# First two chunks of the two 4096-wide feed-forward nets: weights stationary and one tile's 128 tokens moving

## The chip, the cores and the metric

The kernel is one program on one core of a Trainium2 chip. The metric is the device time of one execution in microseconds (us): the median of 3 runs before is 1135.75 us (1135.49 to 1136.52).

The core has a matrix engine (PE in the profile; its weight loads are shown apart, as PEld), a vector engine (DVE), a scalar engine (ACT), GpSimd (POOL) and an engine that issues DMAs (SP). Each takes its own instructions in the order in which the program put them, and waits on semaphores for the others. A matmul multiplies a stationary operand, 128x128, which a weight load brings into the array, by a moving operand of up to 512 columns, and adds the result into a PSUM bank of 128x512 floats.

## The reference, cut to what matters

Three blocks run one after the other on 256 tokens of width 1024, all in float32: a mixer block with a gated net of width 2816, a retention layer, and an attention layer. Retention and attention are each followed by a net of width 4096 with a squared ReLU; these two nets are what the change touches:

```
D_FF_2 = 4 * D_MODEL
def sq_relu_mlp(x, w_up, w_down):
    h = jax.nn.relu(x @ w_up)
    return (h * h) @ w_down
h = h + rms_norm(sq_relu_mlp(rms_norm(h, mpre), w_up, w_down), mpost)
```

## The kernel before

**Split numbers.** Every float32 operand of a large product is split into two rounded parts (type float32r), a high part and the rest. ACT writes the high part, DVE the rest (`split`, L683). A product is then three matmuls, high by high, high by rest and rest by high (`mm3`, L540). The weights come by DMA into `raw` tiles in units of two k-tiles by 512 columns or one k-tile by 1024, 512 KB each; the split puts them into `whi` and `wlo`, of which there are eight buffers each. The activations lie split and transposed (features on the partitions, 256 tokens along the row) in `y8` tiles, named y in the profile. `Parts` (L351) keeps them so that the high and the low part of one k-tile lie side by side.

**Two ways to multiply.** `rows_proj` (L546) has 128 tokens stationary and 512 weight columns moving: 8 k-tiles by three matmuls of 512 columns. Its result has tokens on the partitions, so `rows_T` (L698) transposes it in four 128x128 matmuls against an identity (`const`) and splits it. `cols_proj` (L555) has 128 weight columns stationary; a first matmul moves the high and low parts of all 256 tokens (512 columns) past the high weights, a second moves the high part alone (256 columns) past the rest. Its result is already transposed. `two_blocks` (L564) does two such blocks and adds the two halves.

**The nets.** `run_mlp` (L1223) cuts the 4096 hidden columns into eight chunks of 512. The first two (`ROWS_FIRST`) go through `up` with `token_rows`: for each of the two token tiles (t), for each chunk, a projection by rows, the squared ReLU and the transposes. The reason for the row form there is in the loop: work on tile 0 begins while the input of tile 1 (normalised, transposed and split by `next_T`, L1134) is still being made; `flush()` (L1374) records that before tile 1's work. Chunks 2 to 7 use `two_blocks`. The transposes of the input of tile 1 are matmuls too: 8 of 128x128, in two groups of four.

**What sets the order.** The kernel is recorded twice. In the first pass `Plan` (L69) schedules all operations by its own costs and due times; in the second they are issued in that order, so each engine's queue is fixed. Its cost for a float32r matmul (L197) prices a moving operand of under 256 columns at four times the rate of a wider one:

```
if ins[0].dtype == F32R:
    return n * 0.4167e-3 * (1 if n >= 256 else 4) + 0.0027
```

The kernel before has no float32r matmul of under 256 columns. The four PSUM banks named `mx` are handed out in the order of first use, so the transposes of tile 1's input wait for the first bank that the chunk results leave.

Of the kernel before, what the change touches and what calls it, by code (L numbers as in the profile page):

```python
# [27 lines left out]
AF = mybir.ActivationFunctionType  # L28
OP = mybir.AluOpType
# [4 lines left out]
KT = D // 128  # L34
# [302 lines left out]
class Part:  # L337
# [5 lines left out]
    def __getitem__(self, at):  # L343
        p, k, c = at if len(at) == 3 else (*at, slice(None))
        if isinstance(k, int):
            return self.tiles[k // 4][p, k % 4, self.s, c]
        n = (k.start or 0) // 4
        return self.tiles[n][p, (k.start or 0) - 4 * n:k.stop - 4 * n, self.s, c]


class Parts:  # L351
# [5 lines left out]
    def __getitem__(self, s):  # L357
        if s > 1:
            raise IndexError
        return Part(self.tiles, s)  # L360

    def both(self, k):
        return self.tiles[k // 4][:, k % 4].rearrange("p s n -> p (s n)")
# [3 lines left out]
def network(ctx, tc, I, consts, c_at, out, after=None):  # L367
    nc = tc.nc
    plan = Plan(after)
    V, S, T, G, Q = [Engine(plan, n, e) for n, e in (("DVE", nc.vector), ("ACT", nc.scalar), ("PE", nc.tensor),  # L370
                                                     ("POOL", nc.gpsimd), ("SP", nc.sync))]
# [5 lines left out]
    def sbt(shape, tag, bufs, dt=F32):  # L377
        return plan.tile(sb, shape, dt, tag, bufs)

    def pj():  # L380
        return plan.tile(ps, [128, 512], F32, "pj", 4)

    def mx():
        return plan.tile(ps, [128, 512], F32, "mx", 4)
# [7 lines left out]
    def t2():  # L392
        return sbt([128, 512], "t2", 6)
# [4 lines left out]
    def f32(ap):  # L398
        return ap.bitcast(F32)
# [6 lines left out]
    def cols(a, n):  # L406
        return a.rearrange("p (a b) -> p a b", b=n)
# [93 lines left out]
    def pump(upto):  # L501
        while state["split"] <= min(upto, len(units) - 1) and state["split"] < state["done"] + NSPL:
            i = state["split"]
            load_to(i + NRAW - 1)
            src, kt, n, deint, gain = units[i]
            raw = raws.pop(i)
            hi = sbt([128, UNIT], "whi", NSPL, F32R)[:, :kt * n]
            lo = sbt([128, UNIT], "wlo", NSPL, F32R)[:, :kt * n]
            if deint:
                src4 = raw.rearrange("p (k m c) -> p k c m", k=kt, c=2)  # L510
                hi4, lo4 = [a.rearrange("p (k c m) -> p k c m", k=kt, c=2) for a in (hi, lo)]
                for k in range(kt):
                    S.activation(hi4[:, k], src4[:, k], AF.Copy)
                    V.tensor_tensor(lo4[:, k], src4[:, k], f32(hi4[:, k]), op=OP.subtract)
            elif gain is not None:
                for k in range(kt):
                    split(hi[:, k * n:(k + 1) * n], lo[:, k * n:(k + 1) * n], raw[:, k * n:(k + 1) * n],
                          g_col[:, gain + k:gain + k + 1])
            else:
                split(hi, lo, raw)  # L520
            spl[i] = (cols(hi, n), cols(lo, n))
            state["split"] += 1
        load_to(state["split"] + NRAW - 1)

    def weight(key):
        i = index[key]
        pump(i + AHEAD)
        return spl[i]
# [7 lines left out]
    def release_chunk(key, n):  # L536
        for j in range(n):
            release((key, j))

    def mm3(acc, x, w, first, last):  # L540
        T.matmul(acc, x[0], w[0], start=first, stop=False)
        T.matmul(acc, x[0], w[1], start=False, stop=False)
        T.matmul(acc, x[1], w[0], start=False, stop=last)


    def rows_proj(key, hT, t, acc, c0, n, per=2, nk=KT):  # L546
        for j in range(nk // per):
            w = weight((key, j))
            for k in range(per):
                kk = j * per + k  # L550
                x_ = [a[:, kk, t * 128:(t + 1) * 128] for a in hT]
                mm3(acc, x_, [a[:, k, c0:c0 + n] for a in w], kk == 0, kk == nk - 1)
# [11 lines left out]
    def two_blocks(key, hT, pool, c0, per=2, nk=KT):  # L564
        ps_ = pool(), pool()
        for b, p in enumerate(ps_):
            cols_proj(key, hT, p, c0 + b * 128, per, nk)
        s = cols(t2(), 256)
        for b, p in enumerate(ps_):
            S.activation(s[:, b], p[:, 256:], AF.Copy)  # L570
            V.tensor_tensor(s[:, b], p[:, :256], s[:, b], op=OP.add)
        return s
# [47 lines left out]
    col, n = {}, 0  # L620
# [62 lines left out]
    def split(hi, lo, src, scale=None):  # L683
        if scale is None:
            S.activation(hi, src, AF.Copy)
            V.tensor_tensor(lo, src, f32(hi), op=OP.subtract)
        else:
            S.activation(hi, src, AF.Copy, scale=scale)
            V.scalar_tensor_tensor(lo, src, scale, f32(hi), op0=OP.mult, op1=OP.subtract)

    def new_hT():
        return Parts([y8(), y8()])

    def new_y():
        return Parts([y8()])


    def rows_T(src, dst, k0, t, nb=4, scale=None):  # L698
        p = cols(mx(), 128)[:, :nb]
        for j in range(nb):  # L700
            T.transpose(p[:, j], src[:, j * 128:(j + 1) * 128], ident)
        hi, lo = [a[:, k0:k0 + nb, t * 128:(t + 1) * 128] for a in dst]
        split(hi, lo, p, scale)
# [153 lines left out]
    hT = new_hT()  # L857
# [10 lines left out]
    for key in ("fq", "fk"):  # L868
        heads[key] = cols(p4(), 256)
        acc = pj(), pj()  # L870
        for j in range(4):
            w = weight((key, j))
            for t in range(2):
                for k in range(2):
                    kk = 2 * j + k
# [72 lines left out]
    for t in range(2):  # L948
        p = pj()
# [56 lines left out]
    for t in range(2):  # L1006
        p = pj()
# [12 lines left out]
        for c in range(2 - t):  # L1020
            r = slice(c * 64, (c + 1) * 64)
# [4 lines left out]
        for i in range(2):  # L1026
            r = slice(i * 64, i * 64 + 64)
            V.tensor_copy(qm[r, i::2, t, 0::3], tp[r, :2].rearrange("p a (c n) -> p a c n", c=2))
        tk = slice(t * 128, (t + 1) * 128)
# [15 lines left out]
    for c in range(3):  # L1045
        cs = cols(mx(), 256)
        for pr in range(2):
            T.matmul(cs[:, pr], koz[:, c, pr * 128:(pr + 1) * 128], gv[:, c // 2, pr * 256:(pr + 1) * 256],
                     start=True, stop=True)
        for i in range(2):  # L1050
            r = slice(i * 64, i * 64 + 64)
            if c == 0:
                V.tensor_copy(stt[r, 0], cs[r, :, i * 128:(i + 1) * 128])
            else:
                for pr in range(2):
                    cc = cs[r, pr, i * 128:(i + 1) * 128]
                    V.scalar_tensor_tensor(stt[r, c, pr], stt[r, c - 1, pr], decay[r, 4 * pr + c:4 * pr + c + 1], cc,
                                           op0=OP.mult, op1=OP.add)
    y_gla = new_y()
    for t in range(2):  # L1060
        tk = slice(t * 128, (t + 1) * 128)
        op = mx()
# [15 lines left out]
        for j in range(4):  # L1078
            V.scalar_tensor_tensor(y_gla[1][:, j, tk], tp[:, j], ggla[:, j:j + 1], f32(y_gla[0][:, j, tk]),
                                   op0=OP.mult, op1=OP.subtract)  # L1080
# [5 lines left out]
    for n, i in enumerate(BR):  # L1086
        for c in range(2):
            gt = cols(p4(), 256)
            for b2 in range(2):
                p = two_blocks(("gate", i, c), hT, pj, 256 * b2)  # L1090
# [8 lines left out]
            for b2 in range(2):  # L1099
                p = two_blocks(("br", i, c), ys[i], pj, 256 * b2, nk=4)  # L1100
                g2 = gt[:, 2 * b2:2 * b2 + 2]
                m = mg[c][:, 2 * b2:2 * b2 + 2]
# [5 lines left out]
                if n == 2:  # L1108
                    k = slice(4 * c + 2 * b2, 4 * c + 2 * b2 + 2)
# [62 lines left out]
    def flush():  # L1172
        while later:
            later.pop(0)()

    g_ffn = halves(gain_rows("g_ffn"))
    hT = new_hT()
# [88 lines left out]
    hT = hT_n  # L1266
# [89 lines left out]
    hT = hT_n  # L1356

    def sq_relu(p):  # L1360
        r = t2()
        S.activation(r, p, AF.Relu)
        V.scalar_tensor_tensor(r, p, 0.0, r, op0=OP.max, op1=OP.mult)
        return r

    def sq_up(l):
        key = f"up{l}"

        def up(cs, token_rows):
            aT = {c: new_y() for c in cs}  # L1370
            if token_rows:
                for t in range(2):
                    if t:
                        flush()  # L1374
                    for c in cs:
                        p = mx()
                        rows_proj((key, c), hT, t, p, 0, 512)
                        rows_T(sq_relu(p), aT[c], 0, t)
            else:
                for c in cs:  # L1380
                    for b2 in range(2):
                        p = two_blocks((key, c), hT, mx, 256 * b2)
                        V.scalar_tensor_tensor(p, p, 0.0, p, op0=OP.max, op1=OP.mult)
                        m = slice(2 * b2, 2 * b2 + 2)
                        split(aT[c][0][:, m], aT[c][1][:, m], p)
            for c in cs:
                release_chunk((key, c), 4)
            return aT
        return up
# [16 lines left out]
    hT = hT_n  # L1406
# [62 lines left out]
    hT = hT_n  # L1469
# [56 lines left out]
```

## Time and profile before

| | |
|---|---|
| median of 3 runs | 1135.75 us (1135.49 to 1136.52) |
| the profiled execution, its time | 1135.74 us |
| the profiled execution, first to last instruction (span) | 1134.0 us |
| PE busy | 1124.5 us, 99% |
| DVE busy | 822.3 us, 73% |
| ACT busy | 649.8 us, 57% |
| granted TensorE clock, mean | 0.999 |

The span is what the rows are measured in; 1.7 us of the execution lie outside it. A row of the timeline merges neighbours of one form: start, length from the first start to the last end, form, count. Matmuls are pipelined and each is shown with its latency, so the pace of a series is read from starts, or from a merged row as its length less one matmul's mean duration, divided by the count less one.

### The profile page before, as it was taken

Reading aid. Unit: us, or ns where it says so; the run is one execution under the profiler, and the core shown is the slowest. Engines: PE = TensorE matmul, PEld = TensorE weight load, DVE = VectorE, ACT = ScalarE, POOL = GpSimd, SP = SyncE. Lnnn points to the kernel's source line nnn. Section 1 sums busy time; section 2 is a strip of 40 time slices with the busy share of each in tenths; the row PEclk is TensorE's granted clock in tenths of the full one; section 3 lists DMA queues with packets and bytes.
Section 4 is the critical chain, followed back from the end, with each engine's and each line's share of the span. In section 5 each row is a group of like instructions: output and inputs, shape, how many; then the busy total and the mean of one; then the engine's idle time right before and its main releaser. Section 6 shows DMA issues by size and latency. Waiting matters only on the chain.

```text
span 1134.0 us, 15708 instructions
## 1 busy us (share of the span) xinstructions
PE 1124.5 (99%) x5756; PEld 948.0 (84%) x5756; DVE 822.3 (73%) x1487; ACT 649.8 (57%) x1068; POOL 6.0 (1%) x18
## 2 busy tenths in 40 slices
PE   9999999999999999999999999999999999999997
PEld 7989888888888888888888888888888888888885
DVE  7998797897656566787858497656588889755564
ACT  6867657675645554646556474545466667645451
POOL 1000000000000000000000000000000000000000
PEclk9999999999999999999999999999999999999999
DMA  8654545675666664665464458564637354655631
GB/s 296 222 163 125 165 134 182 220 223 176 205 187 197 186 190 129 201 205 189 150 204 163 130 170 279 167 206 154 217 115 255 117 173 141 225 197 181 215 112 38
DMA packets 100883, 204.22 MB, mean 180 GB/s; under 512 B 6661, under 2 KB 30278, under 8 KB 100806
## 3 DMA queue, kind: packets, MB, share of 16 engines
q1 hardware_dynamic: 99942, 202.17, 55.1%
q10 hardware_dynamic: 864, 1.05, 0.3%
q8 instruction: 45, 0.74, 0.3%
q14 instruction: 32, 0.26, 0.1%
HBM read 202.14 MB, written 1.05 MB: 179 GB/s over the span
## 4 chain that ended last, share of the span: by engine, by line
PE 98%; DVE 1%; DMA 0%; ACT 0%; SPq 0%; issue 0%; DVEq 0%; ACTq 0%
PE pj L213 64%; PE mx L213 34%; DMA raw<-in_w_in_dram 0%; DVE p L213 0%; DVE sm L213 0%; DVE wlo L213 0%; SPq L213 0%; ACT t L213 0%; ACT whi L213 0%; DVE y L213 0%; DVEq L1515 0%; ACTq L213 0%
## 5 line engine op out<-in xcount | busy, mean ns | idle before, releaser
L213 PE MATMUL pj<-whi,y 128*128 128x512 f32 (+2 forms) x1744 | 543.7, 388 | 0.0
L213 DVE TENSOR_TENSOR wlo<-raw,whi 128x1024 fp32r<-128x1024 f32 (+1 forms) x326 | 377.7, 1169 | 125.9 <-ACT whi L213 121.5
L213 ACT ACTIVATE whi<-raw 128x1024 fp32r<-128x1024 f32 (+1 forms) x326 | 326.9, 1018 | 123.2 <-PE pj L213 92.1
L213 PEld LDWEIGHTS pj<-whi,y 128*128 128x128 f32 x1744 | 321.7, 188 | 66.1 <-issue 0.3
L213 PE MATMUL pj<-wlo,y 128*128 128x512 f32 (+2 forms) x872 | 337.4, 387 | 0.7 <-DVE wlo L213 0.6
L213 PE MATMUL mx<-y,whi 128*128 128x512 f32 x672 | 236.8, 396 | 0.0
L213 PEld LDWEIGHTS pj<-wlo,y 128*128 128x128 f32 x872 | 164.0, 188 | 33.5 <-DVE wlo L213 1.8
L213 PE MATMUL mx<-y,wlo 128*128 128x256 f32 x672 | 188.5, 281 | 0.0
L213 PEld LDWEIGHTS mx<-y,whi 128*128 128x128 f32 x672 | 126.1, 188 | 30.0
L213 PE MATMUL pj<-y,whi 128*128 128x512 f32 x416 | 146.4, 396 | 0.0
L213 PEld LDWEIGHTS mx<-y,wlo 128*128 128x128 f32 x672 | 126.5, 188 | 0.9
L213 PE MATMUL pj<-y,wlo 128*128 128x256 f32 x416 | 116.5, 280 | 0.0
L213 PEld LDWEIGHTS pj<-y,whi 128*128 128x128 f32 x416 | 78.1, 188 | 18.2
L213 ACT ACTIVATE t<-mx 128x256 f32<-128x256 f32 (+1 forms) x106 | 41.5, 396 | 83.0 <-PE mx L213 80.4
L213 DVE SCALAR_TENSOR_TENSOR wlo<-raw,gcol,whi 128x512 fp32r<-128x512 f32 (+2 forms) x120 | 85.0, 746 | 5.4 <-ACT whi L213 3.7
L213 ACT ACTIVATE whi<-raw,gcol 128x512 fp32r<-128x512 f32 (+2 forms) x120 | 79.8, 716 | 14.7 <-PE pj L213 10.8
L213 PEld LDWEIGHTS pj<-y,wlo 128*128 128x128 f32 x416 | 78.3, 188 | 0.1
L213 DVE TENSOR_TENSOR t<-mx,t 128x256 f32<-128x256 f32 x88 | 37.0, 421 | 52.3 <-ACT t L213 52.3
L213 PE MATMUL mx<-whi,y 128*128 128x512 f32 x192 | 61.5, 396 | 0.0
L213 ACT ACTIVATE t<-pj 128x256 f32<-128x256 f32 (+1 forms) x74 | 29.7, 402 | 55.5 <-PE pj L213 42.2
L213 ACT ACTIVATE y<-t 128x512 fp32r<-128x512 f32 x33 | 20.9, 632 | 45.0 <-DVE t L213 45.0
L213 PE MATMUL mx<-const,t 128*128 128x128 f32 (+1 forms) x295 | 45.0, 272 | 0.0
(143 smaller groups left out, 839.5 us busy)
## 6 DMA issues: line engine op xcount, KB each, us to landing
raw<-in_w_in_dram SPq DMA_DIRECT2D x115, 512.0 KB, 4.5
raw<-in_w_up_dram SPq DMA_DIRECT2D x64, 512.0 KB, 4.6
raw<-in_w_down_dram SPq DMA_DIRECT2D x64, 512.0 KB, 4.9
raw<-in_w_out_dram SPq DMA_DIRECT2D x32, 512.0 KB, 4.2
raw<-in_w_ffn_down_dram SPq DMA_DIRECT2D x22, 512.0 KB, 3.6
raw<-in_w_ffn_gate_dram SPq DMA_DIRECT2D x18, 512.0 KB, 3.8
raw<-in_w_ffn_up_dram SPq DMA_DIRECT2D x18, 512.0 KB, 5.1
raw<-in_w_branch_dram SPq DMA_DIRECT2D x12, 512.0 KB, 4.7
```

The source lines that it names most:

```text
L213: self.ops[i]()
```

## The change

In the two 4096-wide nets the first two chunks no longer go through `rows_proj` and `rows_T`. A new helper `tile_blocks` takes one token tile and 256 hidden columns: for each of two blocks of 128 weight columns and each of 8 k-tiles, one matmul moves the tile's 128 tokens, high and low part (256 columns), past the high weights, and one moves the high part alone (128 columns) past the rest. Both blocks share one PSUM bank. ACT then copies one half out, DVE adds the other, squares with the ReLU, and the result is split; there are no transposes. The helper is called twice for each chunk and tile. The gated net is not touched, nor are chunks 2 to 7.

```diff
+    def parts(self, k):
+        return self.tiles[k // 4][:, k % 4]
...
-    def sq_relu(p):
-        r = t2()
-        S.activation(r, p, AF.Relu)
-        V.scalar_tensor_tensor(r, p, 0.0, r, op0=OP.max, op1=OP.mult)
-        return r
+    def tile_blocks(key, c, b2, t, y):
+        tk = slice(t * 128, (t + 1) * 128)
+        p = mx().rearrange("p (b s n) -> p b s n", b=2, s=2)
+        for b in range(2):
+            c0 = 256 * b2 + 128 * b
+            for kk in range(KT):
+                wb = [a[:, kk % 2, c0:c0 + 128] for a in weight(((key, c), kk // 2))]
+                T.matmul(p[:, b], wb[0], hT.parts(kk)[:, :, tk], start=kk == 0, stop=False)
+                T.matmul(p[:, b, 0], wb[1], hT[0][:, kk, tk], start=False, stop=kk == KT - 1)
+        u = cols(t2()[:, :256], 128)
+        S.activation(u, p[:, :, 1], AF.Copy)
+        V.tensor_tensor(u, p[:, :, 0], u, op=OP.add)
+        V.scalar_tensor_tensor(u, u, 0.0, u, op0=OP.max, op1=OP.mult)
+        m = slice(2 * b2, 2 * b2 + 2)
+        split(y[0][:, m, tk], y[1][:, m, tk], u)
...
                     for c in cs:
-                        p = mx()
-                        rows_proj((key, c), hT, t, p, 0, 512)
-                        rows_T(sq_relu(p), aT[c], 0, t)
+                        for b2 in range(2):
+                            tile_blocks(key, c, b2, t, aT[c])
```

The planned order of the queues changes with it. On PE, at the first of the two nets, the transposes of tile 1's input (here from t2_1173 and t2_1174) stood after 34 matmuls of 512 columns, eight together with the first four of the chunk result (t2_1168). Before:

```order
L213 MATMUL mx_86<-whi_1162,y8_1110 128x512 [waits Activation_49]
L213 MATMUL mx_86<-wlo_1163,y8_1110 128x512 [waits DVE_49]
L213 MATMUL mx_86<-whi_1162,y8_1110 128x512 x2
L213 MATMUL mx_83<-const_64,t2_1173 128x128 [waits DVE_49]
L213 MATMUL mx_83<-const_64,t2_1173 128x128 x3
L213 MATMUL mx_90<-const_64,t2_1168 128x128 x4
L213 MATMUL mx_86<-wlo_1163,y8_1110 128x512
```

After, at the same place (the same transposes now read t2_1175 and t2_1176):

```order
L213 MATMUL mx_90<-y8_1111,whi_1153 128x256
L213 MATMUL mx_90<-y8_1111,wlo_1154 128x128
L213 MATMUL mx_83<-const_64,t2_1175 128x128 [waits DVE_49]
L213 MATMUL mx_83<-const_64,t2_1175 128x128 x3
L213 MATMUL mx_90<-y8_1111,whi_1153 128x256
L213 MATMUL mx_90<-y8_1111,wlo_1154 128x128
```

The first group now stands after 42 matmuls (16 pairs into bank mx_83 and 5 pairs into mx_90), and the second group follows 10 matmuls, or 5 pairs, later; both go into mx_83. In the second net the counts are the same, 42 and 10.

On DVE, the same place in the first net: the queue that ends the making of tile 1's input and then takes the first chunk result out of bank mx_83. Before:

```order
L213 SCALAR_TENSOR_TENSOR t2_1173<-t2_1173,sm_1180,p4_1094 128x512 [waits DVE_49]
L213 SCALAR_TENSOR_TENSOR t2_1174<-pj_97,sm_1180,p4_1092 128x512
L213 TENSOR_TENSOR t2_1174<-t2_1174,p4_1094 128x512 [waits DVE_49]
L213 SCALAR_TENSOR_TENSOR t2_1168<-mx_83,t2_1168 128x512 [waits Activation_49]
L213 TENSOR_TENSOR wlo_1170<-raw_1152,whi_1169 128x1024 [waits DMAHW1_49,PE_49]
L213 TENSOR_TENSOR p4_1144<-p4_1144,p4_1090 128x1024
```

After:

```order
L213 SCALAR_TENSOR_TENSOR t2_1175<-t2_1175,sm_1182,p4_1094 128x512 [waits DVE_49]
L213 SCALAR_TENSOR_TENSOR t2_1176<-pj_97,sm_1182,p4_1092 128x512
L213 TENSOR_TENSOR t2_1176<-t2_1176,p4_1094 128x512 [waits DVE_49]
L213 TENSOR_TENSOR t2_1168<-mx_83,t2_1168 128x256 [waits Activation_49]
L213 TENSOR_TENSOR wlo_1171<-raw_1152,whi_1170 128x1024 [waits DMAHW1_49]
L213 SCALAR_TENSOR_TENSOR t2_1168<-t2_1168 128x256 [waits DVE_49]
L213 TENSOR_TENSOR y8_1110<-mx_83,y8_1110 128x4x128 [waits Activation_49]
```

The operation that empties mx_83 (t2_1168<-mx_83) still stands behind the same three operations on tile 1's input; it is half as wide, and one weight split and the square stand between it and the operation that empties mx_83 a second time (y8_1110<-mx_83).

## Rows read from the trace of the kernel before

**Rows 1.** The page: span, PE's busy time, and the chain's shares by engine.

```profile
span 1134.0 us, 15708 instructions
PE 1124.5 (99%) x5756; PEld 948.0 (84%) x5756; DVE 822.3 (73%) x1487; ACT 649.8 (57%) x1068; POOL 6.0 (1%) x18
...
PE 98%; DVE 1%; DMA 0%; ACT 0%; SPq 0%; issue 0%; DVEq 0%; ACTq 0%
```

**Rows 2.** The chain in order of time, first net: start us, us, what.

```profile
655.32 36.10 PE mx L213 x184
691.41 22.12 PE pj L213 x96
```

**Rows 3.** Timeline of PE, the first net's row stage: start us, us, form, count.

```profile
655.15 0.39 PE L213 MATMUL mx<-whi,y 128*128 128x512 f32 x1
...
663.01 1.04 PE L213 MATMUL mx<-const,t 128*128 128x128 f32 x8
...
665.98 0.60 PE L213 MATMUL mx<-const,t 128*128 128x128 f32 x4
...
666.65 0.62 PE L213 MATMUL mx<-whi,y 128*128 128x512 f32 x2
...
679.60 0.39 PE L213 MATMUL mx<-y,whi 128*128 128x512 f32 x1
```

**Rows 4.** Busy us (x instructions) in both nets' row stages; the second's first matmul.

```profile
655.16:679.60 24.44, 24.44 (x118) 19.95 (x117) 23.28 (x42) 18.20 (x31) 0.00 (x0) 1.00 0.43 141
945.51:969.90 24.39, 24.39 (x118) 20.02 (x116) 23.49 (x40) 17.31 (x31) 0.00 (x0) 1.00 0.47 150
...
945.51 0.40 PE L213 MATMUL mx<-whi,y 128*128 128x512 f32 x1
```

**Rows 5.** Timeline of PE: float32r matmuls of 256 columns back to back.

```profile
92.52 0.27 PE L213 MATMUL pj<-wlo,y 128*128 128x256 f32 x1
...
93.34 0.28 PE L213 MATMUL pj<-whi,y 128*128 128x256 f32 x1
```

**Rows 6.** PE, 128 moving columns (plain float32): a timeline row, then all by form.

```profile
123.50 1.05 PE L213 MATMUL mx<-y,p 128*128 128x128 f32 x8
...
L213 PE MATMUL mx<-y,p 128*128 128x128 f32 x16 | 2.1, 275 | 0.0
```

**Rows 7.** Weight loads by form (busy us, mean ns), then two neighbours in the timeline.

```profile
L213 PEld LDWEIGHTS pj<-whi,y 128*128 128x128 f32 x1744 | 321.7, 188 | 66.1 <-issue 0.3 <-ACT whi L213 0.3
L213 PEld LDWEIGHTS mx<-const,t 128*128 128x128 f32 x294 | 36.0, 140 | 8.3 <-DVE t L213 1.0
...
649.74 0.19 PEld L213 LDWEIGHTS pj<-whi,y 128*128 128x128 f32 x1
649.85 0.19 PEld L213 LDWEIGHTS pj<-wlo,y 128*128 128x128 f32 x1
```

**Rows 8.** Timeline of DVE, first net, while tile 1's input is made.

```profile
661.61 0.69 DVE L213 TENSOR_TENSOR t<-t,p 128x512 f32<-128x512 f32 x1
662.22 0.68 DVE L213 SCALAR_TENSOR_TENSOR t<-mx,t 128x512 f32<-128x512 f32 x1
662.82 1.21 DVE L213 TENSOR_TENSOR wlo<-raw,whi 128x1024 fp32r<-128x1024 f32 x1
663.95 1.22 DVE L213 TENSOR_TENSOR p<-p,p 128x1024 f32<-128x1024 f32 x1
```

**Rows 9.** Timeline of DVE, the same place of the second net.

```profile
945.90 0.68 DVE L213 TENSOR_TENSOR y<-mx,y 128x512 fp32r<-128x512 f32 x1
...
952.15 0.69 DVE L213 SCALAR_TENSOR_TENSOR t<-mx,t 128x512 f32<-128x512 f32 x1
```

**Rows 10.** DVE and ACT by form: busy us, mean ns, idle before.

```profile
L213 DVE TENSOR_TENSOR t<-mx,t 128x256 f32<-128x256 f32 x88 | 37.0, 421 | 52.3 <-ACT t L213 52.3
...
L213 DVE TENSOR_TENSOR y<-mx,y 128x512 fp32r<-128x512 f32 x44 | 29.7, 684 | 4.1 <-ACT y L213 4.0
...
L213 ACT ACTIVATE t<-mx 128x256 f32<-128x256 f32 x96 | 35.6, 375 | 75.3 <-PE mx L213 75.3
```

## The prediction

> **What bounds the kernel now.** I read the page first. PE is busy for 99% of the span, and the chain that ends last runs on PE for 98% [rows 1]: whatever PE has to do more or less of goes straight into the time, and work of the other engines counts only where PE waits for it. So the case is one of PE's pace in two short stretches, and of the waits that a new order brings there.
>
> The stretches are the row stages of the two wide nets, 24.44 and 24.39 us, both with PE filled to the end at the full granted clock (1.00, the 2.4 GHz level) [rows 4]. What fills them can be counted. 96 matmuls of 512 columns take 22.12 us, or 0.2304 each [rows 2]. Four transposes with one such matmul behind them take 666.65 - 665.98 = 0.67 us, so the four alone 0.44 [rows 3]. In the first stage stand 96 matmuls and 20 transposes: 22.12 + 5 x 0.44 = 24.32 of 24.44 us. There is next to no wait to win. DVE is busy for 23.28 of these 24.44 us [rows 4], close behind, but PE does not wait for it.
>
> **What it removes.** For each net 96 matmuls of 512 columns, 22.12 us, and 16 transposes (four of them after the stage), 4 x 0.44 = 1.76. Together 23.88 us on the path.
>
> **What it adds on PE.** For each net 2 chunks x 2 tiles x 4 blocks x 8 k-tiles = 128 pairs: a matmul of 256 columns and one of 128, each with a weight load of its own.
>
> The 256: seven back to back take 93.34 - 92.52 = 0.82 us, 0.117 each [rows 5].
>
> The 128 is what decides, and the trace has none in this type. Bounds from the nearest rows: at the low end half of the 256, 0.058 (columns alone count); at the high end the 0.2304 of a 512 [rows 2], which is the planner's assumption of a quarter of the rate. Between them stands the nearest real row, the plain float32 matmuls of 128 columns with a load each: eight in 1.05 us, one lasting 275 ns, so (1.05 - 0.275) / 7 = 0.111 each [rows 6]. I take this value, for the load speaks for it whatever the moving side can do: two loads of this type, neither held up by a long matmul, start 649.74 and 649.85, that is 0.11 apart [rows 7], and I take it that a load hides behind one matmul, the one before its own. Behind a 256 (0.117) it just fits; behind a 128 it does not. So the change moves as many columns as before (128 x 384 = 96 x 512) in 256 loads instead of 96, and half of these loads set the pace.
>
> A pair is then 0.117 + 0.111 = 0.228 us, 128 pairs 29.18, and each net's stage grows by 29.18 - 23.88 = 5.3 us. Both: **+10.6 us**.
>
> The Trainium skill speaks against this change in the same sense: "TensorE: Matmul & The Clock Gate", section "LDWEIGHTS (loading the stationary operand)", has a load take as long as its columns at 1.2 GHz, 107 ns for 128 by its formula, whatever moves. The trace agrees with its 0.11 [rows 7]; by the page's figure in place of 0.111 the growth would be an estimated 4.8 us a net instead of 5.3.
>
> **The new order's waits.** The queues are fixed by a plan that prices the 128 at four times its width, so the plan reaches each point later than PE will. The first transposes of tile 1's input now stand after 42 matmuls, 21 pairs: at my pace 4.79 us into the stage, at 655.15 + 4.79 = 659.94 [rows 3]. They need bank mx_83, which DVE empties only behind the three operations on tile 1's input; these do not get shorter, since they start from the previous layer's last product. In the trace DVE gets past them at 662.22, empties the bank in 0.68 us to 662.90, and the transposes begin at 663.01 [rows 3, 8], with no gap on PE, because 34 matmuls of 0.23 had brought it there at the same moment. Now the emptying takes 0.42 [rows 10]: 662.22 + 0.42 + 0.11 = 662.75. PE waits **2.8 us**, and all that is queued behind the transposes on PE waits with it.
>
> The second group goes into the same bank, 5 pairs later: PE is there at 662.75 + 0.44 + 1.14 = 664.33. Before it DVE has a weight split, the square (256 wide) and the split of the first group: with neighbours overlapping by some 0.07 [rows 8], 662.22 + 0.35 + 1.13 + 0.35 + 0.68 = 664.73, and 664.84 with the hand-over. **0.5 us**.
>
> Second net: the upper half of tile 0's input is needed after 4 pairs (945.51 + 0.91 = 946.42 [rows 4]) where 12 long matmuls stood before; DVE ends it at 946.58 [rows 9], so 0.3 us with the hand-over. Then 945.51 + 0.3 + 4.79 = 950.6 against 952.15 + 0.42 + 0.11 = 952.68 [rows 9, 10]: 2.1. The second group as above: 0.5. In all 3.3 us in the first net and 2.9 in the second, **+6.2 us**. This is an estimate from rows of an order that is no longer there; if DVE frees the bank earlier the waits go to 0, and at worst I give them half as much again.
>
> **What costs nothing.** Emptying and splitting a chunk result costs DVE more: three operations of 0.42 for half a chunk (2.5 for a whole one) instead of 0.68 + 0.68 [rows 10], about 1.2 x 4 = 4.6 us a net, and ACT some 1.4. DVE then has 23.3 + 4.6 = 27.9 us of work in a stage of 29.2 + 3.3 = 32.5; without that slack (a pair under 0.19) PE would begin to wait for it. The weight buffers come free later, since every unit is read four times and not once for each tile; between the last read of chunk 0 and the start of chunk 2 lie some 9 us, in which ACT and DVE have four splits of 1.1 to do. The DMAs of the weights have the same bytes to bring in more time.
>
> **Sum.** The profiled execution took 1135.74 us, at the median (1135.75). 1135.74 + 10.6 + 6.2 = **1152.5 us**. With no waits it is 1146.3; with waits of 9 and a pair dearer by 0.01 (256 x 0.01 = 2.6), 1158.
>
> **The rivals.**
>
> *A quarter of the rate.* The 128 streams no faster than a 512. For it: no row has this type at this width, so nothing excludes it, and the planner's cost assumes it. The 0.111 is also for one of the two instructions into which a plain float32 product falls (16 rows for the kernel's 8 such products [rows 6]). Against it: the assumption has no row behind it either. Priced as both of those instructions, 2 x 0.111 = 0.222: 128 x 0.339 = 43.4, less 23.88, is 19.5 a net, 39.0 in both. PE then reaches the transposes at 655.15 + 7.12 = 662.27, so the waits shrink to some 0.5 in all: 1175.2. At 0.2304 it is 1176.9.
>
> *The load hides further.* The loads of transposes are shorter (140 ns against 188) [rows 7]; were this type's so too, a pair would near 0.117 + 0.058 = 0.175, 22.4 us a net, 3.0 less in both. But PE would be at the first transposes at 658.8 and wait 3.9 us, then 0.9; second net 4.4: -3.0 + 9.2, and DVE becomes the bound for another 1 or 2 us: 1143. So even the low end of the matmul's cost is slower than before. Against it: the two loads 0.11 apart. The skill's page has a rule to this side (section "Back-to-back issue gap"): 81 ns for a matmul of 128 in a stream with loads. By it I estimate 1147.
>
> *Not slower.* The low end, 0.175 a pair, and bank mx_83 free when PE asks, because the emptying is reached earlier than at 662.22. That gives 1135.74 - 3.0 = 1132.7. It decides from a pair of 0.187 with no wait at all (23.88 / 128), and needs both that DVE skips a chain which the order keeps and that a load takes under 0.07. Very little speaks for it.
>
> **How the numbers follow.** Load-bound pairs with waits: 0.61, 1152.5, itself 1146 to 1158. A quarter of the rate: 0.30, 1175 to 1177. The load hides: 0.06, 1143. Not slower: 0.03, 1132.7. The likeliest gives the time. The first two hold 0.91; to hold 8 in 10 the range has to reach the second, so it runs from 1145 to 1177. About 0.2% (2.3 us) is what a measurement can tell from no change. All cases but the last are slower by more; of its 0.03, two thirds faster and one third same, and a little more for same from waits and pairs both at their low ends: faster 0.02, same 0.02, slower 0.96.
>
> **What would show it.** Right: 128 matmuls of each width in each of the two stages, starts 0.11 to 0.12 apart throughout, weight loads at the same pace, stages of about 32.5 and 32.1 us, and one gap on PE of 2 to 3 us before the first transposes, put down to DVE. Wrong in the size of the 128: starts 0.22 or more behind each of them, a stage of some 44 us and no gap (A quarter), or 0.06 to 0.08 (the load hides). Wrong in the waits: no gap, with the bank emptied before 660. Everything outside the stages should keep its length, 22.12 us for the 96 matmuls behind among it.

## The result

The changed kernel took 1155.67 us at the median of 4 runs (1153.81 to 1156.45), the kernel before beside it 1136.13 (1135.49 to 1137.36): 1.0168 times as long, interval 1.0156 to 1.018, or 19.5 us. A second set of runs gave 1155.33 against 1135.97. The forecast was 1152.5, range 1145 to 1177, slower with a chance of 0.96. The sign and the mechanism of the pairs held. The median lies 3.2 us above the forecast, and most of these 3.2 us have a cause that the prediction did not name at all, a fall of PE's clock; the experiments isolate it.

The profiled execution of after is the quickest of the four: 1153.81 us, span 1151.8 against 1134.0.

### The profile page after: what moved, and what is told of

The parts are those of the page before. It is cut to its first block, busy times and chain, and to the rows that moved or that the text cites. A ratio compares the mean times of both kernels' runs of the same rounds, so it can differ in the third digit from the quotient of the medians.

```text
span 1151.8 us, 16343 instructions
## 1 busy us (share of the span) xinstructions
PE 1137.8 (99%) x6044; PEld 969.8 (84%) x6044; DVE 832.4 (72%) x1519; ACT 651.4 (57%) x1084; POOL 5.9 (1%) x18
## 4 chain that ended last, share of the span: by engine, by line
PE 94%; DVE 2%; DMA 2%; ACT 1%; SPq 0%; issue 0%; DVEq 0%; ACTq 0%
PE pj L213 61%; PE mx L213 33%; DMA const<-consts_dram 1%; DVE wlo L213 1%; DVE t L213 1%; DMA raw<-in_w_in_dram 1%; DMA p<-in_ln_mlp_post_dram 1%; SPq L213 0%; DVE p L213 0%; ACT whi L213 0%; DVE sm L213 0%; DMA x<-in_x_dram 0%; ACT t L213 0%; DVE y L213 0%; DVEq L1528 0%
## 5 line engine op out<-in xcount | busy, mean ns | idle before, releaser
L213 PE MATMUL mx<-y,whi 128*128 128x512 f32 (+1 forms) x928 | 297.6, 380 | 0.1
L213 PE MATMUL mx<-y,wlo 128*128 128x256 f32 (+1 forms) x928 | 245.9, 265 | 0.0
L213 PEld LDWEIGHTS mx<-y,whi 128*128 128x128 f32 x928 | 175.2, 189 | 30.5 <-DVE y L213 0.4
L213 PEld LDWEIGHTS mx<-y,wlo 128*128 128x128 f32 x928 | 176.4, 190 | 0.7
L213 DVE TENSOR_TENSOR t<-mx,t 128x256 f32<-128x256 f32 x104 | 43.7, 421 | 53.2 <-ACT t L213 53.2
L213 ACT ACTIVATE y<-t 128x512 fp32r<-128x512 f32 (+1 forms) x49 | 27.5, 562 | 69.1 <-DVE t L213 69.1
L213 PE MATMUL mx<-const,t 128*128 128x128 f32 (+1 forms) x263 | 41.2, 275 | 4.7 <-DVE t L213 4.4
L213 PEld LDWEIGHTS mx<-const,t 128*128 128x128 f32 (+1 forms) x263 | 32.4, 141 | 12.5 <-DVE t L213 5.6
```

The costliest lines, as they stand in the source:

```text
L213: self.ops[i]()
```

## The profile after

The page of after, the lines that answer to [rows 1]: span, busy time, the chain's shares by engine.

```profile
span 1151.8 us, 16343 instructions
PE 1137.8 (99%) x6044; PEld 969.8 (84%) x6044; DVE 832.4 (72%) x1519; ACT 651.4 (57%) x1084; POOL 5.9 (1%) x18
...
PE 94%; DVE 2%; DMA 2%; ACT 1%; SPq 0%; issue 0%; DVEq 0%; ACTq 0%
```

PE is busy for 13.3 us more, and the span is 17.8 longer: some 4.5 us are new idle time of PE. The chain shows that PE waits, but not for how long: it now leaves PE for DVE, DMA and ACT for 5 or 6% of the span, where it was 1 or 2, and beside most of that work PE was busy.

Where it grew: I cut each wide net from its first `mx` matmul to the first of the 96 `pj` products behind the chunks, 36.10 us before in the first net [rows 2, with its start in rows 3] and 36.03 in the second. These two pieces in after, busy us (x instructions) of PE, PEld, DVE, ACT, POOL, then the granted clock, the DMA share and GB/s:

```profile
655.25:699.65 44.40, 41.85 (x329) 40.14 (x328) 38.77 (x74) 24.23 (x48) 0.00 (x0) 1.00 0.48 163
953.89:999.34 45.45, 43.52 (x329) 41.82 (x329) 37.14 (x72) 24.53 (x49) 0.00 (x0) 0.96 0.42 140
```

+8.30 and +9.42, together 17.7 of the span's 17.8. The rest of the program kept its length. The second net's 0.96 in the clock column is the thing to notice; it comes up below.

The pairs. PE's timeline in the first net, start us, us, form, count, and in brackets the idle time before and what ended it:

```profile
655.25 0.28 PE L213 MATMUL mx<-y,whi 128*128 128x256 f32 x1
655.37 0.22 PE L213 MATMUL mx<-y,wlo 128*128 128x128 f32 x1
655.42 0.34 PE L213 MATMUL mx<-y,whi 128*128 128x256 f32 x1
655.59 0.22 PE L213 MATMUL mx<-y,wlo 128*128 128x128 f32 x1
...
659.96 0.22 PE L213 MATMUL mx<-y,wlo 128*128 128x128 f32 x1
662.42 0.66 PE L213 MATMUL mx<-const,t 128*128 128x128 f32 x4 [2.23 <-DVE t L213]
...
664.49 0.66 PE L213 MATMUL mx<-const,t 128*128 128x128 f32 x4 [0.32 <-DVE y L213]
```

From the first 128 (655.37) to the twenty-first (659.96, 20 pairs on) are 4.59 us, 0.2295 a pair. Behind the first pair the 128 starts 0.17 after its 256, and the next 256 0.05 to 0.06 after the 128. The weight loads in the same stretch stand at an even pace:

```profile
656.97 0.19 PEld L213 LDWEIGHTS mx<-y,whi 128*128 128x128 f32 x1
657.08 0.19 PEld L213 LDWEIGHTS mx<-y,wlo 128*128 128x128 f32 x1
657.20 0.19 PEld L213 LDWEIGHTS mx<-y,whi 128*128 128x128 f32 x1
657.31 0.19 PEld L213 LDWEIGHTS mx<-y,wlo 128*128 128x128 f32 x1
```

Then PE stands still before the first transposes of tile 1's input: from 659.96 to 662.42, 2.46 us from start to start, some 2.35 of them over the pace; and half a microsecond before the second group. DVE, on the same clock:

```profile
661.33 0.69 DVE L213 TENSOR_TENSOR t<-t,p 128x512 f32<-128x512 f32 x1
661.94 0.42 DVE L213 TENSOR_TENSOR t<-mx,t 128x256 f32<-128x256 f32 x1
...
663.75 0.69 DVE L213 TENSOR_TENSOR y<-mx,y 128x512 fp32r<-128x512 f32 x1
```

The operation at 661.94 empties bank mx_83; it ends at 662.36, and the transposes start at 662.42. They wait for the bank, behind the making of tile 1's input, as the order said. The one at 663.75 empties it the second time and ends at 664.44, and the second group starts at 664.49.

The second net does the same, and then something else. PE's timeline there:

```profile
958.93 0.22 PE L213 MATMUL mx<-y,wlo 128*128 128x128 f32 x1
961.03 0.66 PE L213 MATMUL mx<-const,t 128*128 128x128 f32 x4 [1.87 <-DVE t L213]
...
962.33 0.52 PE L213 MATMUL mx<-y,whi 128*128 128x256 f32 x1
962.65 0.31 PE L213 MATMUL mx<-y,wlo 128*128 128x128 f32 x1
962.75 0.52 PE L213 MATMUL mx<-y,whi 128*128 128x256 f32 x1
```

A wait of 2.1 us, and 1.3 us after its end a pair takes 962.75 - 962.33 = 0.42 instead of 0.23, with nothing in brackets. Read the clock column (behind the five engines' busy time) of the windows around it:

```profile
958.90:961.10 2.20, 0.33 (x4) 0.18 (x3) 2.17 (x5) 1.25 (x3) 0.00 (x0) 1.00 0.68 250
...
962.00:963.00 1.00, 1.00 (x7) 1.00 (x6) 1.00 (x4) 0.74 (x2) 0.00 (x0) 0.50 0.00 0
963.00:964.00 1.00, 1.00 (x7) 1.00 (x6) 1.00 (x3) 0.00 (x0) 0.00 (x0) 0.50 0.90 152
...
966.00:967.00 1.00, 1.00 (x11) 1.00 (x11) 1.00 (x3) 0.39 (x1) 0.00 (x0) 1.00 0.00 0
```

During the wait the granted clock still reads 1.00. From about 961.95 to 965.4 (3.4 us) it is 0.50, the 1.2 GHz level, though PE is busy throughout, and then 1.00 again. 7 matmuls fit into a microsecond there instead of 11. In the first net of this execution the clock did not fall. The page's row of PE's clock in 40 slices shows nines throughout; a slice of 29 us hides a fall of 3.4.

## Experiments

Two theories for the whole. **Mine**: the pair is bound by weight loads at 0.228 us (+10.6), the plan puts PE before a bank that DVE empties later (+5 in waits), and the waits bring PE to half its clock for a few microseconds (+1.5 to 4.5). **Rivals**: the 128 is dear for its columns; the waits alone make up all that is not pairs; the extra work of DVE and ACT costs time elsewhere.

### The same kernel once more

Nothing edited.

> The changed kernel as it is, once more, for the granted clock of each run. Theory (pairs that the weight load paces, +10.6; PE's wait for the first transposes, about +5; and a fall of the granted clock after that wait, +1.4 and more): again about 1155.7 us, and the runs spread along the clock, about 1153.8 at 0.998 and 1155.5 to 1156.5 at 0.994 to 0.995. Rival (the clock has no part in it, the rest is dearer work): no tie between a run's clock and its time.

1155.33 us (1153.81 to 1157.56), ratio 1.0172 (1.0158 to 1.0186). The profiled execution was the slowest, 1157.56, so that it can be held against the quickest above. Windows of its two falls:

```profile
665.20:671.50 6.30, 6.30 (x30) 6.30 (x31) 5.43 (x8) 2.28 (x4) 0.00 (x0) 0.50 0.30 84
965.30:968.40 3.10, 3.10 (x18) 3.10 (x17) 2.98 (x5) 1.02 (x3) 0.00 (x0) 0.51 0.50 118
```

Here the clock fell in both nets; read in windows of 0.25 us, for 6.8 us (664.97 to 671.8) and for 3.4 us (965.34 to 968.75). The chain (start us, us, what) of the first net in the execution of after above, from the second group of transposes to the end of the chunks:

```profile
664.49 35.33 PE mx L213 x272
699.82 22.12 PE pj L213 x96
```

and the same piece of the same kernel in this one:

```profile
665.20 38.38 PE mx L213 x272
703.57 22.12 PE pj L213 x96
```

The same 272 instructions, 3.05 us more: that is what 6.8 us at half clock cost. The mean granted clock of each run fits: 0.998 in the quickest of both sets (1153.81 us in either), 0.994 to 0.996 in the six others. Outside the two nets the clock is at 0.50 in these executions, and in that of before, only within the last 3 us of the program.

### The wait filled

Eight matmuls of 512 columns, which nobody reads, on PE ahead of the first transposes of tile 1 in each wide net; everything else in the order of after.

```diff
+                if fill:
+                    bank, w, some = pj(), weight(((fill[0], 0), 0))[0], []
+                    for _ in range(8):
+                        T.matmul(bank, hT[0][:, 0, :128], w[:, 0], start=True, stop=True)
...
+                        some.append(len(plan.ops) - 1)
+                    plan.moves.append((some, len(plan.ops)))
```

> The changed kernel with 8 matmuls of 512 columns (1.84 us) put on PE right ahead of the first transposes of tile 1's input, into a PSUM bank that nobody reads: work without use, in the place of the wait; every other queue as in the changed kernel. Theory: the 8 cost nothing, since PE waits 2.0 to 2.5 us there anyway, and since PE no longer idles the clock does not fall: 1152 us (1151 to 1153.5), clock 0.998 or more in every run. If the clock has nothing to do with the wait: as the changed kernel, 1155.7. If the wait is not one for DVE's queue, but something in front of PE: 3.7 us more, 1159.

1152.66 us (1152.52 to 1152.77), ratio 1.0147 (1.0133 to 1.016): with 1.84 us more of work in each net the kernel is 2.7 us quicker. PE's timeline in the first net, where 2.46 us of standing still have become 0.84 from start to start:

```profile
659.90 2.04 PE L214 MATMUL pj<-whi,y 128*128 128x512 f32 x8
...
662.39 0.66 PE L214 MATMUL mx<-const,t 128*128 128x128 f32 x4 [0.45 <-DVE t L214]
```

and the windows of both nets, with the clock at 1.00 (behind the engines' busy time):

```profile
655.00:675.00 20.00, 19.23 (x158) 18.38 (x157) 19.17 (x31) 8.49 (x18) 0.00 (x0) 1.00 0.49 170
956.00:976.00 20.00, 19.68 (x163) 18.89 (x162) 17.68 (x44) 8.26 (x22) 0.00 (x0) 1.00 0.27 84
```

The transposes start when they did (662.39 and 662.42, from stages that start at 655.13 and 655.25): the filling is paid for by the wait. What it takes away is the fall of the clock. No pair, no DVE operation and no gate differs from after, and the first net, where the clock did not fall in after's profiled execution, is as long as there (44.50 and 44.40). So the 2.7 us are the clock's, and the runs no longer scatter (0.25 us instead of 3.75). The two pieces are 44.50 and 44.39 us long here, 16.8 above before: the prediction's sum without its missing term.

### The wait made longer

Four more additions on DVE, 1.72 us in all by the trace (some 1.35 had been expected), ahead of the operation that empties mx_83, in each net.

```diff
+        if c == 0 and b2 == 0 and t == 0:
+            some = []
+            for _ in range(4):
+                V.tensor_tensor(tt[:, 256:], x[:, 0, :256], x[:, 0, :256], op=OP.add)
...
+                some.append(len(plan.ops) - 1)
+            plan.moves.append((some, len(plan.ops)))
```

> The changed kernel with four DVE operations of 128x256 (about 1.35 us together, results unused) put right ahead of the one that empties the first chunk result's bank, in each of the two nets; every other queue as in the changed kernel. Theory: PE's wait for the first transposes grows from 2.0 to 2.5 to about 3.5 to 3.9 us, and the clock falls in both nets in every run: 2.8 us from the wait and 1 to 4 more from the clock, 1159 to 1162 us, clock 0.995 or less throughout. If the clock hangs on something else: 1158.5 and clocks spread as before. If the wait is not for this DVE operation: 1155.7.

1160.2 us (1160.14 to 1161.05), ratio 1.0216 (1.0202 to 1.023), 4.9 above after. Windows of the waits and of what follows them, first net, then second:

```profile
660.65:665.00 4.35, 0.23 (x3) 0.08 (x2) 4.18 (x10) 1.65 (x3) 0.00 (x0) 0.92 0.77 276
665.00:670.80 5.80, 5.80 (x28) 5.80 (x29) 5.30 (x7) 2.44 (x4) 0.00 (x0) 0.50 0.33 97
...
963.84:967.60 3.76, 0.22 (x2) 0.07 (x1) 3.62 (x9) 1.20 (x3) 0.00 (x0) 1.00 0.48 173
968.10:971.20 3.10, 3.10 (x17) 3.10 (x16) 3.07 (x5) 1.01 (x2) 0.00 (x0) 0.50 0.46 144
```

Of the lengthening, 1.9 and 1.7 us are wait (4.34 and 3.79 us from start to start against 2.46 and 2.09); the rest, 1.3 us, is put down to the clock. A fall comes with both waits, of 6.8 and 3.4 us. The first begins inside its wait, at 664.3, 0.7 us before PE is released, which is why the window of that wait reads 0.92. The mean clock of the five runs, 0.992 to 0.995, fits falls in each. DVE gates PE nearly one for one, and the clock adds to it.

### The 128 priced as it runs

The planner's price of a float32r matmul under 256 columns: its load instead of four times its columns. The floor also lifts the price of a 256-column matmul, from 0.1094 to 0.1107 us. Nothing else; the order follows.

```diff
-                return n * 0.4167e-3 * (1 if n >= 256 else 4) + 0.0027
+                return max(n * 0.4167e-3, 0.108) + 0.0027
```

> The changed kernel with one line of the planner altered: a float32r matmul of 128 columns is priced at 0.111 us, as the trace now shows, in place of 0.216. The matmuls are the same; the order is planned for their real pace, so tile 1's transposes stand further back on PE. Theory: the waits go, and with them the fall of the clock; the pairs stay: 1136.1 + 10.6 = 1146.7 us, 1146 to 1148, clock 0.998 or more in every run, weight loads still 0.11 apart. Rival (the blocks cost more than their pace, on DVE, ACT or by the clock of a stage with short matmuls): 1152 or more.

1146.65 us (1146.31 to 1147.08), ratio 1.0094 (1.008 to 1.0108). In the trace 61 and 62 matmuls of the stage stand before the first transposes, where it was 42. In the first net PE still waits, for 1.27 us from start to start:

```profile
662.37 0.66 PE L213 MATMUL mx<-const,t 128*128 128x128 f32 x4 [0.94 <-DVE t L213]
```

In the second it does not wait at all, and the chain there is one piece:

```profile
951.23 41.64 PE mx L213 x328
992.87 22.13 PE pj L213 x96
```

with PE busy for all of it (window of the second net, busy us of PE, PEld, DVE, ACT, POOL behind its length):

```profile
951.07:992.71 41.64, 41.64 (x330) 40.20 (x330) 36.62 (x72) 24.31 (x49) 0.00 (x0) 1.00 0.47 153
```

In neither net does the clock fall. Nearly half of after's loss was the order's. The rest is mainly the pairs: this second net is the cleanest measurement of them, 41.64 - 36.03 = +5.6 us without a wait and at full clock (forecast 5.3).

### The price line by itself

The same line in the kernel before, to see what of the last run came from places that the change does not touch. That kernel has no float32r matmul under 256 columns, so only the lift of the 256s is at work here.

> The kernel before, with the planner's price line of e1_priced (a float32r matmul under 256 columns at the time of its load, 0.108 us, instead of four times its columns). This measures what of e1_priced comes from that line alone, away from the two changed stages: in e1_priced's trace the later chunks of the wide nets take 11.14 + 11.09 where the kernel after has 11.25 + 11.07, 0.09 x some 6 in each net, and the start up to the first net is 1 us earlier. Theory: the line is worth 0 to 1.5 us elsewhere, so this runs at 1134.5 to 1136 and the growth of e1_priced from the changed stages alone is 10.7 to 12. Rival: the line does nothing outside the changed stages: 1136.1, and the earlier start of e1_priced is chance.

1135.19 us (1134.34 to 1135.95, 11 runs) against 1136.17 (20 runs), ratio 0.9989 (0.998 to 0.9999): about 1 us quicker. The chain of a later chunk reads

```profile
714.57 11.14 PE mx L213 x64
725.71 11.09 PE pj L213 x48
```

where the trace of before has 11.25 and 11.07. Ten such chunks give 0.9 us (the first net's row stage gives 0.5 of it back here, in a wait of 0.75 us before the transposes). So the kernel of the last run has 0.9 us from places that the change does not touch: its two pieces are 42.70 and 41.64 us long, 12.2 above before, where the median grew by 10.7. (Its profiled execution also came to the first `mx` matmul of the program at 271.06; the ten others come at 271.7 to 272.9, three with the same price line among them.) These 12.2 are the pairs, at 5.6 a net, and the wait of 1.2 left in the first.

### The 128 made as wide as the 256

The order of the run with the new price, and the second matmul of each pair also takes 256 columns.

```diff
-                T.matmul(p[:, b, 0], wb[1], hT[0][:, kk, tk], start=False, stop=kk == KT - 1)
+                T.matmul(p[:, b], wb[1], hT.parts(kk)[:, :, tk], start=False, stop=kk == KT - 1)
```

> As e1_priced, but the second matmul of each pair moves 256 columns and not 128: the low part of the tile is moved past the rest of the weights as well (a fourth product that the split leaves out otherwise, added in; the sum is if anything closer). 256 matmuls of twice the width, not one load more. Theory (the load sets the pace of the narrow one, 0.111 us, and a 256 takes 0.117): 256 x 0.006 = 1.5 us over e1_priced, 1148.2. Rival (columns set the pace and something else filled e1_priced's pairs): 256 x 0.058 = 15 us over it, 1161.5.

1148.17 us (1147.55 to 1148.61), ratio 1.0104 (1.009 to 1.0118): 1.5 us above the run it is built on. The second net's chain:

```profile
952.43 42.51 PE mx L213 x328
994.93 22.13 PE pj L213 x96
```

42.51 - 41.64 = 0.87 us for 128 matmuls of twice the width, 0.007 each. This is the experiment on which the reading of the pair rests: columns are all but free there, so a 128 is paid for its load. (In the first net both pieces are 42.70 long, since a wait of 1.2 us takes the difference in. The stages explain 0.9 of the 1.5 us. This execution reached the first `mx` matmul of the program at 272.18, as before did at 272.15; it is the run with the new price that was early there, by 1.1 us, in a part that the edit does not touch.)

### Only the first net changed

```diff
-                        for b2 in range(2):
-                            tile_blocks(key, c, b2, t, aT[c])
+                        if l == 0:
+                            for b2 in range(2):
+                                tile_blocks(key, c, b2, t, aT[c])
+                        else:
+                            p = mx()
+                            rows_proj((key, c), hT, t, p, 0, 512)
+                            rows_T(sq_relu(p), aT[c], 0, t)
```

> The change in the first of the two wide nets alone; the second as in the kernel before. Theory: the first stage as in the changed kernel, +8.3 us with the clock undisturbed and about +3 more where it falls: 1144.3 to 1147.5, clock 0.996 to 0.999, and the second stage back at 36.0 us from its first matmul to the products behind. If the two nets shared a cost (a buffer or a DMA that runs late from the first into the second): half of 19.4 would not be met, and the second stage would not be 36.0.

1146.12 us (1144.68 to 1147.43), ratio 1.0086 (1.0073 to 1.01): +9.95, half of after's 19.5. The second net is back at its old length:

```profile
956.55 36.03 PE mx L213 x184
992.58 22.12 PE pj L213 x96
```

Nothing is carried from one net to the other. In the first, this execution has a wait of 3.46 us from start to start, 1.0 longer than in after (the section on the prediction says why), and a fall of 3.4 us; its piece is 46.64 long, +10.5.

### Chunk 1 with both tiles' columns

From the kernel before: chunk 0 stays in rows, chunk 1 goes through blocks whose four banks stay open over both tiles, so that the second matmul of a k-tile moves both tiles' high parts at once. All matmuls have 256 columns, three for each k-tile and block instead of four.

```diff
+                    if not t:
+                        held = [cols(q, 256) for q in (mx(), pj(), pj(), mx())]
...
+                            T.matmul(held[j][:, :, tk], wb[0], hT.parts(kk)[:, :, tk],
+                                     start=not t and kk == 0, stop=False)
+                            if t:
+                                T.matmul(held[j][:, 0], wb[1], hT[0][:, kk], start=False, stop=kk == KT - 1)
```

> The kernel before with chunk 1 alone in another form: its four blocks of 128 weight columns stationary keep their PSUM banks from tile 0 to tile 1; tile 0 moves 256 columns (its high and low part) past the high weights, tile 1 the same, and one matmul moves the high parts of both tiles, 256 columns, past the rest. So every weight load stands beside a matmul of 256. Theory (a load costs nothing beside 256 columns): for each net 96 matmuls of 256, 96 x 0.117 = 11.23 us, in place of 48 of 512 and 8 transposes, 11.06 + 0.88 = 11.94: 0.7 us less a net, 1.4 in both, 1134.6 against 1136.0. Rival (short matmuls cost more than their columns, or the banks that are held make the transposes of tile 1's input wait): 1136 or more, with a gap on PE in front of those transposes.

1135.51 us (1135.01 to 1137.0, 11 runs) against 1136.17, ratio 0.9995 (0.9986 to 1.0004): not told from no change. In the trace its two pieces are 35.56 and 35.52 us long, 0.5 below before in each net, where 0.7 had been expected.

And with the price line on top:

> e5_held (chunk 1 in blocks whose banks stay open across both tiles, so that all its matmuls have 256 moving columns) with the same price line. Theory: the two add up, -0.7 and 0 to -1.5 us against 1136.1: 1134 to 1135.5, faster than both kernels by about the bound of the measurement. Rival: neither is real, 1136.

1134.64 us (1133.35 to 1135.73, 11 runs), ratio 0.9985 (0.9976 to 0.9994). PE's timeline in chunk 1:

```profile
672.35 0.28 PE L213 MATMUL mx<-y,whi 128*128 128x256 f32 x1
672.47 0.29 PE L213 MATMUL mx<-y,wlo 128*128 128x256 f32 x1
672.59 0.28 PE L213 MATMUL mx<-y,whi 128*128 128x256 f32 x1
```

Starts 0.12 apart: load and columns are in balance. This is the quickest kernel of the study, by 1.5 us or 0.15%; the interval leaves out no change, but the size is under the 0.2% that I said one measurement can tell.

## Why the prediction was right, and what it missed

**The pair: right.** Forecast 0.117 + 0.111 = 0.228, measured 0.2295; +5.3 us a net forecast, +5.6 in the clean net. The reason given, that the load of a 128 sets the pace, is shown by the doubled width at 0.007 us. The picture behind it was a little off: I expected starts 0.11 to 0.12 apart throughout. The loads do stand so; the matmuls start 0.17 and 0.06 apart in turn. The Trainium skill, "TensorE: Matmul & The Clock Gate", section "LDWEIGHTS (loading the stationary operand)", gives a load of 128 columns 107 ns whatever moves, and the loads 0.11 to 0.12 apart agree. The section "Back-to-back issue gap" of that page of the Trainium skill, by which I had estimated 1147 with 81 ns for a matmul of 128, is not borne out for these float32r matmuls: beside a 256 at 0.117 [rows 5] the 128 takes 0.2295 - 0.117 = 0.112 us.

**A quarter of the rate (0.30): wrong.** The 128s would have had to take 0.22 or more. This case is why the range went up to 1177, 21 us above the result. The plain float32 rows 0.111 apart were the better witness than the planner's constant, and I could have trusted them more.

**The load hides (0.06), not slower (0.03): wrong.** The pairs keep to 0.23, and the bank was not empty when PE came.

**The waits: right in place and nearly in size; of the cause one step was wrong.** In the profiled execution of after:

| wait | forecast us | measured us |
|---|---|---|
| first net, first transposes | 2.8 | 2.35 |
| first net, second group | 0.5 | 0.48 |
| second net, tile 0's upper half | 0.3 | 0.2 |
| second net, first transposes | 2.1 | 2.0 |
| second net, second group | 0.5 | 0 (PE comes late, at half clock; 0.48 with the wait filled) |
| sum | 6.2 | 5.0 |

The largest miss is DVE, which reached the emptying of mx_83 at 661.94, 0.28 earlier than in the order of before [rows 8], on which the estimate stood. The prediction took the operations on tile 1's input to start from the previous layer's last product. In the first net they start from a DMA. ACT makes the row sums that they need, and in its queue stands, ahead of the sums, an operation on the gains of the norm behind this net (`in_ln_mlp_post`), which are needed only later; ACT waits for their transfer. ACT's row in before, then the chain in after (start us, us, what), then in the run with only the first net changed:

```profile
655.63 1.06 ACT L213 ACTIVATE p<-p 128x1024 f32<-128x1024 f32 x1 [0.56 <-DMA p<-in_ln_mlp_post_dram]
...
649.07 6.26 DMA p<-in_ln_mlp_post_dram
...
649.31 7.32 DMA p<-in_ln_mlp_post_dram
```

The transfer lands at 655.33 in after and at 656.63 in the other run. ACT starts that operation at 655.63, 655.36 and 656.65, and DVE comes to the bank 6.58 or 6.59 us later in all three (662.22, 661.94, 663.24). So the first net's wait is set by when this transfer lands against PE's start of the stage, 655.25 and 655.54: hence 2.46 us in the one run and 3.46 in the other, and the wait of 1.27 that the new price left, where PE began at 654.27 and ACT at 655.32. No run moved the transfer, so what the wait would be without it is not shown. In the second net the chain goes back to products on PE, as forecast.

The third row is not 0.3 but a start 0.28 us after the one before it, where 0.06 is the pace.

**What costs nothing: right.** In the second net of the run with the new price PE has no gap in 41.64 us while DVE is busy for 36.6 of them, so DVE's and ACT's extra operations are covered; the 96 products behind keep their 22.12 us, and no weight comes late in that piece.

**The missing term: the clock.** The prediction read the granted clock, 1.00 in both stages [rows 4], and kept it there. It priced a wait of PE as the time in which PE stands still. In fact six of the seven waits of 2.1 to 4.3 us that the traces show came with 3.4 or 6.8 us at half clock, nearly all of them with PE busy: 1.5 and 3 us more. The 1.5 is worked out from the second net: 45.45 us in after against 44.39 with the wait filled, or 1.06, to which the 0.5 of the second group's wait comes that the slower PE no longer meets; the 3.05 is read from the two chains above. So the profiled execution is 11.0 to 11.2 of pairs (128 x 0.2295 - 23.88 a net, or 5.6), 5.0 of waits and 1.5 of clock, against a span 17.8 longer; the six executions at a lower mean clock took 1.5 to 3.75 us more. With the wait filled, and so without this term, the kernel takes 1152.66, and the prediction said 1152.5. That agreement is partly luck: the pairs cost some 0.6 more and the waits some 0.7 less than forecast.

The Trainium skill, "TensorE: Matmul & The Clock Gate", section "HAM oscillation — how this bites in real kernels", warns that a kernel which lets PE idle between bursts of matmuls loses its clock. The windows at 0.50 behind waits of 2.1 us agree in kind; the idle times of its example are longer than these. The clock should have stood in the prediction as a term beside the waits, since these were in the forecast.

**What stays open.** The runs show that the fall comes with the waits and goes when they are filled (0.84 us left) or short (1.27). They do not show why the wait of 2.46 us had no fall where one of 2.07 had, nor why a fall lasts 6.8 us with waits of 2.79 and 4.34 and 3.4 us with waits of 2.07, 2.10, 3.46 and 3.79. I did not vary the wait finely enough to say from what length it happens.

## What to carry to other kernels

Count weight loads as well as moving columns: on PE a float32r matmul with a load of its own cost 0.11 us here, so 128 moving columns cost nearly what 256 do, and a layout that gets rid of transposes by narrowing the moving side pays for it. A planner's price that is wrong in either direction puts other engines' gates in the wrong place; when an operation is new to a planner, check its price against the trace first (that one line took 8.7 us off the 19.5, 0.9 of them in other chunks). And where an edit makes PE wait as long as here, some 2 us, price the wait with a spell at half clock behind it, and look at the clock in windows of a microsecond, since the slices of the profile's page hide it. When a wait is forecast, follow its chain to the start: an operation that nobody needs yet can stand in an engine's queue ahead of one that everybody waits for.

## What the runs showed of the hardware that I had not expected

- In five of the six falls the granted clock fell only after PE had gone back to work, 0.5 to 1.8 us behind waits of 2.1 to 3.8 us through which it read 1.00. In the longest wait, 4.34 us, it fell 0.7 us before PE resumed.
- In the first net, from ACT's start on the gains of a later norm to DVE's emptying of the bank are 6.58 to 6.59 us in eight executions, wherever the transfer lands; with the four additions it is 8.30.
- Useless matmuls in the waits made the kernel 2.7 us quicker and its runs agree within 0.25 us.
- In a stream of alternating 256s and 128s the loads run evenly and the matmuls do not (0.17 and 0.06), and doubling the columns of a load-bound matmul costs 0.007 us.
